# Layer 1's input projection: block sums of the token operand taken once in full precision, the token pairs in another order, and the products of a query group added straight from the accumulators

## The chip, the cores and the metric

The kernel runs on one NeuronCore of a Trainium2 chip. A core has a matrix engine (PE), a vector engine (DVE), an activation engine (ACT), a general-purpose engine (POOL) and a synchronisation engine (SP) that here issues nearly all transfers. Each engine works its own list of instructions in order; an instruction waits until what it reads is written and what it overwrites has been read. The metric is the device time of one execution in microseconds (us), the median of several.

## The reference, cut to what matters

Two layers run over 1024 latent tokens and 256 context tokens of width 1024. Layer 0 is windowed attention, layer 1 is multi-head latent attention. The change is in layer 1's input projection alone:

```python
hx = rms_norm(x, norm_g[i]) * (1.0 + scale_x[:, None]) + shift_x[:, None]
hc = rms_norm(ctx, norm_g[i]) * (1.0 + scale_c) + shift_c
...
cq, ckv, kr, g = jnp.split(h @ w_in, [B_Q_LORA, B_Q_LORA + B_KV_LORA, ...], axis=-1)
q  = (rms_norm(cq, q_norm) @ w_uq).reshape(b, n, B_HEADS, B_NOPE + B_ROPE)
kv = (rms_norm(ckv, kv_norm) @ w_ukv).reshape(b, n, B_HEADS, B_NOPE + B_V)
```

Everything is fp32. `h @ w_in` has 512 columns `cq` and 1024 columns of gate `g`, wanted for the latent tokens alone, and 256 + 32 columns `ckv` and `kr`, wanted for all 1280 tokens.

## The kernel before

**Products.** An fp32 operand is held as two rounded parts, high and low. `split` makes them: ACT casts the high part (L125), DVE or POOL subtracts it for the low part (L126). A product of two such operands is three matmuls, high by high, low by high and high by low (L130, L131, L132).

**The tiles.** The 1280 tokens are ten tiles of 128, in five pairs: pair 0 is context, pairs 1 to 4 are latent. For a pair, `norm_x` loads two tiles, takes their squares' sum on ACT (L231), the power on POOL (L233) and scales on DVE (L234); `turn_h` transposes on PE (L245), writes the shifted and scaled result in fp32 to a transposed tile `xt` (ACT, L249) and splits it (L253, L254) into the pair's part of `hT1`. `xt` comes from a ring of two buffers, `xtr`.

**The kv stage.** `kv_tile` runs 24 matmuls of 128x288 for a tile, then ACT squares (L1026), DVE forms the mean (L1027), POOL takes the power -1/2 (L1028), and DVE scales the result (L1064). Two tiles later PE transposes it (L1077), it is split and stored (L1081).

**The block products.** `cq` and `g` are worked out by a scheme of Strassen's kind (Winograd's form): the weight columns come in six groups of 256 (`groups`: 0 and 1 are `cq`, 2 to 5 are `g`), and a group is seven products P1 to P7 instead of eight. A product is 12 matmuls of 128x512 into one of eight PSUM banks. P1 and P2 use raw blocks on both sides (the token side is `halves`, which lies over `hT1`); P6, P5, P7 and P4 use sums of token blocks T2, T1, T3, T4 against S2, S1, S3 and the raw block A22; P3 uses S4. `Group.op` makes the weight side (sums on DVE, L1146 to L1160, then a split with the low part on POOL), and `Group.P` issues the products and their combination.

`t_sums` makes the token side: for pairs 1 and 3 behind tile 6 and for pairs 2 and 4 behind tile 8, each a quarter-set of 128x1024. It reads pair 3's or 4's fp32 `xt` and the high and low parts of pair 1's or 2's `hT1`:

```python
nc.vector.tensor_sub(X, X, a[0])          # L1099
nc.vector.tensor_sub(X, X, a[1])          # L1100
nc.vector.tensor_sub(Y, Y, X)             # L1101
put(T2, Y, nc.vector)                     # high L1096 (ACT), low L1097
put(T1, X, nc.gpsimd)
nc.gpsimd.tensor_sub(X, Y, a[0])          # L1104
nc.gpsimd.tensor_sub(X, X, a[1])          # L1105
...
nc.gpsimd.tensor_sub(Y, b[0], Y)          # L1109, later
nc.gpsimd.tensor_add(Y, Y, b[1])          # L1110
```

**After a product.** P1 is copied out (ACT, L1174), P6 added to it (DVE, L1180); P7 and P5 are copied to buffers (ACT, L1184 and L1188) and added there by POOL (L1189, L1190); P4 and P3 are added from their banks by DVE (L1195, L1200). `post` then applies silu and stores to `g1_d` (L1207, L1208), or stores to `cq_d` (L1213) and collects squares (ACT L1215 or L1218, POOL L1219) in `sqacc`.

**The norm of cq.** `latent_rms` sums the squares over the columns by matmuls (L1224), takes the mean (DVE, L1228) and the power (POOL, L1229) and spreads it by transposes (L1234). `latent_rows` loads `cq` again (L1242) and scales it (L1243). Then `qr_tile` (transposes L1260, stores L1264) and `qn_tile` (L1281 to L1285) make the queries; they share buffers (`qst`, `stg`, `ev`) with the weight loads of the stages around them, the last of these `b_w_ukv` (L1388). The rotary key is made there too (L1424 to L1432). From then on the attention units run.

**What sets the order.** The program is written in one stream; a scheduler of the framework, with costs of its own, makes from it a fixed list for each engine. Buffers are offsets in KB in three areas (`F`, `R`, and `arena_k` for the upper part of `R`), so two uses of one offset also order the instructions.

## Time and profile before

| what | value |
|---|---|
| time, median of 3 runs | 1603.81 us (1602.33 to 1604.04) |
| the profiled execution's own time | 1606.34 us |
| its span, first to last instruction | 1604.6 us (1.74 us lie outside) |
| granted PE clock, mean | 0.98 |
| PE busy | 1535.8 us, 96% of the span |
| DVE, ACT, POOL busy | 1040.7, 806.3, 851.2 us |

Layer 1's input projection, with the cq norm and the queries, lies between about 705 and 1000 us of the span. The profile's stretches show for each engine how long it was busy in each, with the granted clock of PE; a row of waits names the engine, the line, what it waited for, the sum, the count and the longest.

### The profile page before, as it was taken

The page shows a single profiled execution, that of the slowest core. Times are in us where ns is not written, and L with a number is a line of the kernel's source. Part 1 is how long each engine was busy: PE and PEld are TensorE (multiplying, and loading weights), DVE is VectorE, ACT ScalarE, POOL GpSimd, SP SyncE. Part 2 cuts the span into 40 slices and gives each one's busy share as a digit, 9 for nine tenths or more (in the row PEclk, how much of TensorE's full clock was granted, in tenths as well). Part 3 has the DMA queues.
Part 4 walks back from the last instruction along what each step waited for, and adds up shares of the span by engine and source line. Part 5 has one row for each costly group of instructions (what it writes and reads, how often), then busy time and mean ns, then how long its engine had stood idle before and what let it go on. Part 6 is the DMA issues. An engine that isn't in the chain of part 4 may idle for free. (4 is left out here: it accounts for less than half of the span.)

```text
span 1604.6 us, 25745 instructions
## 1 busy us (share of the span) xinstructions
PE 1535.8 (96%) x9190; PEld 1194.6 (74%) x9190; DVE 1040.7 (65%) x1748; ACT 806.3 (50%) x1552; POOL 851.2 (53%) x873
## 2 busy tenths in 40 slices
PE   7999999999999999998698999999999999999998
PEld 4988888887888888878577777666766766766587
DVE  3868996557777777766543442667677677667354
ACT  4333222377777777768433433455555555555321
POOL 1152212136554444544877562588688688689510
PEclk9999999999999999999798999999999999999999
DMA  9347673654343333245133477222333233244151
GB/s 329 101 155 226 193 209 118 205 145 112 93 135 96 93 97 92 80 146 169 40 112 121 148 244 244 93 76 86 81 88 90 67 95 96 67 129 117 62 170 66
DMA packets 157967, 204.01 MB, mean 127 GB/s; under 512 B 14592, under 2 KB 91904, under 8 KB 157840
## 3 DMA queue, kind: packets, MB, share of 16 engines
q1 hardware_dynamic: 156368, 200.48, 41.7%
q10 hardware_dynamic: 1472, 1.90, 0.4%
q8 instruction: 72, 1.18, 0.3%
q14 instruction: 55, 0.45, 0.1%
HBM read 151.46 MB, written 50.87 MB: 126 GB/s over the span
## 5 line engine op out<-in xcount | busy, mean ns | idle before, releaser
L130 PE MATMUL PB<-arena_r 128*128 128x512 f32 (+2 forms) x990 | 371.7, 377 | 11.7 <-ACT arena_r L125 5.0
L1568 POOL TENSOR_TENSOR arena_f<-arena_f 128x512 f32<-128x512 f32 x252 | 328.3, 1303 | 82.2 <-ACT arena_f L1560 65.4
L131 PE MATMUL PB<-arena_r 128*128 128x512 f32 (+2 forms) x958 | 355.0, 371 | 4.7 <-POOL arena_r L126 3.5
L132 PE MATMUL PB<-arena_r 128*128 128x512 f32 (+2 forms) x926 | 340.1, 368 | 0.0
L126 POOL TENSOR_TENSOR arena_r<-arena_f,arena_r 128x512 fp32r<-128x512 f32 x110 | 147.2, 1350 | 282.4 <-ACT arena_r L125 236.9
L130 PEld LDWEIGHTS PB<-arena_r 128*128 128x128 f32 x990 | 189.3, 192 | 48.4 <-ACT arena_r L125 6.5
L1560 ACT ACTIVATE arena_f<-PB 128x1024 f32<-128x1024 f32 x160 | 164.1, 1026 | 109.6 <-PE PB L1554 69.2
L1519 DVE TENSOR_REDUCE arena_f<-PB 128x1 f32<-128x1024 f32 x128 | 156.0, 1218 | 86.5 <-PE PB L1517 86.4
L131 PEld LDWEIGHTS PB<-arena_r 128*128 128x128 f32 x958 | 183.6, 192 | 34.1 <-POOL arena_r L126 4.0
L132 PEld LDWEIGHTS PB<-arena_r 128*128 128x128 f32 x926 | 177.1, 191 | 28.9 <-issue 1.7
L1554 PE MATMUL PB<-arena_r 64*128 64x512 f32 (+1 forms) x1490 | 194.5, 392 | 0.3 <-ACT arena_f L1560 0.3
L1554 PEld LDWEIGHTS PB<-arena_r 64*128 64x128 f32 (+1 forms) x1490 | 135.8, 185 | 29.1 <-ACT arena_f L1560 1.8
L126 DVE TENSOR_TENSOR arena_r<-PB,arena_r 128x512 fp32r<-128x512 f32 (+1 forms) x171 | 115.6, 684 | 60.7 <-ACT arena_r L125 60.0
L1576 PE MATMUL PB<-arena_f 128*64 128x512 f32 x640 | 144.4, 597 | 0.0
L628 DVE CUSTOM_DVE_ANT_0 arena_f<-PB,arena_f,small 128x640 f32<-128x640 f32 (+2 forms) x176 | 125.0, 721 | 20.0 <-PE PB L617 13.3
L631 ACT ACTIVATE arena_f<-arena_f,small 128x640 f32<-128x640 f32 (+2 forms) x160 | 119.5, 747 | 35.1 <-DVE small L628 32.1
L125 ACT CAST arena_r<-arena_f 128x512 fp32r<-128x512 f32 (+1 forms) x139 | 83.7, 618 | 86.5 <-DMA arena_f<-b_w_ukv 18.2
L125 ACT CAST arena_r<-PB 128x512 fp32r<-128x512 f32 (+1 forms) x171 | 98.1, 581 | 46.5 <-PE PB L648 44.2
L617 PE MATMUL PB<-arena_k,arena_r 128*128 128x256 f32 (+1 forms) x576 | 112.0, 309 | 2.5 <-DVE small L628 1.3
L648 PE MATMUL PB<-ident,arena_f 128*128 128x128 f32 x672 | 104.6, 275 | 1.1 <-DVE arena_r L126 0.7
L1576 PEld LDWEIGHTS PB<-arena_f 128*64 128x64 f32 x640 | 43.1, 136 | 83.2 <-issue 79.7
L617 PEld LDWEIGHTS PB<-arena_k,arena_r 128*128 128x128 f32 x576 | 89.8, 189 | 15.2 <-DVE small L628 3.7
(253 smaller groups left out, 2693.0 us busy)
## 6 DMA issues: line engine op xcount, KB each, us to landing
arena_f<-ada_w SPq DMA_DIRECT2D x40, 512.0 KB, 4.8
arena_r<-q_d SPq DMA_DIRECT2D x80, 256.0 KB, 3.9
arena_r<-qn_d SPq DMA_DIRECT2D x64, 256.0 KB, 4.1
arena_r<-qr_d SPq DMA_DIRECT2D x170, 64.0 KB, 3.4
arena_f<-a_w_in SPq DMA_DIRECT2D x40, 256.0 KB, 3.1
g_d<-arena_f SPq DMA_DIRECT2D x32, 256.0 KB, 2.8
q_d<-arena_f SPq DMA_DIRECT2D x64, 128.0 KB, 2.5
arena_f<-b_w_in SPq DMA_DIRECT2D x16, 512.0 KB, 3.8
```

What stands on the lines that cost most here:

```text
L125: nc.scalar.copy(hi, src)
L126: (lo_eng or nc.vector).tensor_sub(lo, src, hi.bitcast(F32))
L130: nc.tensor.matmul(o, ah, bh, start=first, stop=False, skip_group_check=more)
L131: nc.tensor.matmul(o, al, bh, start=False, stop=False, skip_group_check=more)
L132: nc.tensor.matmul(o, ah, bl, start=False, stop=last, skip_group_check=more)
L617: nc.tensor.matmul(S[:, at : at + n], qT[:, s, hq, :], kT[:, g, k : k + n], start=s == 0, stop=s == 1)
L628: nc.vector.tensor_tensor_reduce(P[:, a:b], S[:, 256 + a : 256 + b], mk, 1.0, sk, ALU.add, ALU.min, to)
L1519: nc.vector.reduce_max(mx[:, 32 + b : 33 + b], flat, AX.X, negate=True)
L1554: nc.tensor.matmul(S[:, t], k[r, c : c + 128], q[r], start=j == 0, stop=j == 4)
L1560: nc.scalar.activation(E, self.S, AF.Exp)
L1568: eng.tensor_add(self.acc, self.acc, E[:, t])
L1576: nc.tensor.matmul(self.pv[p : p + 64], Vq[:, cs[t], self.h % 4, :], E[:, t], start=i == 0, stop=i == 4)
```

## The change

- **Pairs.** The kv stage takes the pairs in the order 0, 1, 3, 2, 4. The sums of pairs 1 and 3 are written behind the fourth tile, those of pairs 2 and 4 behind the eighth. Pair 2's `xt` takes the buffer of pair 1's, pair 4's that of pair 3's.
- **Sums.** They are taken from two fp32 `xt`, one subtraction each (L1093, L1094, L1095, L1102), high parts on ACT (L1098), low parts on DVE (L1099). POOL has no part in them. T4's split comes later, as before.
- **First products.** P1 and P2 of groups 0 and 1, which need no sums, stand ahead of all products that do; those of groups 2 and 3 stand inside the kv stage, as before. The weight side runs eight products ahead (six before), and loads for P1 and P2 alone fetch half.
- **Combination.** Within a group the order is 6, 5, 7, 4, 3. DVE adds P5 and P7 straight from their banks (L1177); the ACT copies and the POOL adds are gone.
- **The norm of cq.** `latent_rms` stands behind group 4's second product (before: group 2's second). The loads of `cq` (L1226) are written ahead of the scaling (L1232), which is split by halves of the tokens.
- **Weights and buffers.** The last query weights' low parts go to DVE; `stg` has five slots there that share nothing with `qst`; many offsets in `F` are others.

By number the lines behind it move up: L1027 and L1028 become L1026 and L1027, L1064 L1065, L1077 L1078, L1174 L1165, L1180 L1171, L1195 and L1200 L1185, L1219 L1205, L1224 to L1234 L1210 to L1220. The lists of PE hold the same matmuls in another order; ACT's has 26 rows fewer, POOL's 30 fewer, DVE's 18 more.

POOL at the end of the kv stage. In the names, `arena_f` and `arena_r` are the areas, `small` holds one value per token, `krF` the rotary key. Before:

```order
L126 TENSOR_TENSOR arena_r<-arena_f,arena_r 128x512
L1097 TENSOR_TENSOR arena_r<-arena_f,arena_r 128x4x256
L1104 TENSOR_TENSOR arena_f<-arena_f,arena_r 128x1024
L1105 TENSOR_TENSOR arena_f<-arena_f,arena_r 128x1024
L1028 TENSOR_TENSOR small<-small 128x1
L291 TENSOR_TENSOR krF<-krF,arena_f 128x32
L1109 TENSOR_TENSOR arena_f<-arena_r,arena_f 128x1024
L126 TENSOR_TENSOR arena_r<-arena_f,arena_r 128x512
L1028 TENSOR_TENSOR small<-small 128x1
L1110 TENSOR_TENSOR arena_f<-arena_f,arena_r 128x1024
```

And at the same place of the change:

```order
L126 TENSOR_TENSOR arena_r<-arena_f,arena_r 128x512
L1027 TENSOR_TENSOR small<-small 128x1
L291 TENSOR_TENSOR krF<-krF,arena_f 128x32
L1027 TENSOR_TENSOR small<-small 128x1
L291 TENSOR_TENSOR krF<-krF,arena_f 128x32
L126 TENSOR_TENSOR arena_r<-arena_f,arena_r 128x512 x4
L1027 TENSOR_TENSOR small<-small 128x1
L291 TENSOR_TENSOR krF<-krF,arena_f 128x32
```

The sums between the powers are gone; ahead of the power of the ninth tile stand four low parts of weights.

DVE at the same place of the change, from the second set of sums on:

```order
L1094 TENSOR_TENSOR arena_f<-arena_f 128x1024
L1099 TENSOR_TENSOR arena_r<-arena_f,arena_r 128x4x256
L1095 TENSOR_TENSOR arena_f<-arena_f 128x1024
L1099 TENSOR_TENSOR arena_r<-arena_f,arena_r 128x4x256
L1102 TENSOR_TENSOR arena_f<-arena_f 128x1024
L1099 TENSOR_TENSOR arena_k<-arena_f,arena_k 128x4x256
L1026 TENSOR_SCALAR small<-small 128x1
L126 TENSOR_TENSOR arena_k<-PB,arena_k 128x256
L1065 SCALAR_TENSOR_TENSOR arena_f<-PB,small,arena_f 128x256
L281 TENSOR_TENSOR krF<-PB,arena_f 128x32
L286 TENSOR_TENSOR arena_f<-PB,arena_f 128x2x8 x2
L1099 TENSOR_TENSOR arena_k<-arena_f,arena_k 128x4x256
```

Six of the sums' instructions stand in a row ahead of the mean (L1026) and the scaling (L1065) of one tile, and another low part ahead of the next tile's.

POOL around the power for the cq norm, before (L1229) and now (L1215):

```order
L1219 TENSOR_TENSOR arena_f<-arena_f 128x512
L126 TENSOR_TENSOR arena_r<-arena_f,arena_r 128x512
L1219 TENSOR_TENSOR arena_f<-arena_f 128x512
L126 TENSOR_TENSOR arena_r<-arena_f,arena_r 128x512
L1229 TENSOR_TENSOR small<-small 128x8
```

```order
L126 TENSOR_TENSOR arena_r<-arena_f,arena_r 128x512
L1205 TENSOR_TENSOR arena_f<-arena_f 128x512
L126 TENSOR_TENSOR arena_r<-arena_f,arena_r 128x512 x12
L1215 TENSOR_TENSOR small<-small 128x8
L126 TENSOR_TENSOR arena_r<-arena_f,arena_r 128x512 x9
```

Between the last sum of squares and the power stood one low part; now there are twelve.

The core of the diff:

```diff
@@ -986,21 +986,20 @@
-    xtr = Ring(F, [22, 30], 2048)
-    ev = Ring(F, [2, 4, 6, 8], 512)
...
-    cmb = Ring(F, [10 + 2 * i for i in range(6)], 512)
...
-    stg = Ring(F, [42, 44.25, 49.5], 576)
...
+    xr = Ring(F, [22, 26, 45], 1024)
+    xtr = Ring(F, [14, 37], 2048)
+    wr = Ring(F, [30, 32], 512)
...
+    ov = Ring(F, [34, 45, 47, 4, 6], 512)
...
+    stg = Ring(F, [30, 32.25, 49.5], 576)
@@ -1085,45 +1086,35 @@
-    def t_sums(p, xt):
...
+    def t_sums(x0, x1, cs, t4):
+
+        la, lb, ha, hb = x0[:, 0:4], x0[:, 4:8], x1[:, 0:4], x1[:, 4:8]
+        sub = nc.vector.tensor_sub
+        sub(la, ha, la)
+        sub(ha, hb, ha)
+        sub(hb, hb, la)
+
+        def put(T, src):
             nc.scalar.copy(T[:, 0, :, cs], src)
...
+            sub(T[:, 1, :, cs], src, T[:, 0, :, cs].bitcast(F32))
+
+        put(T2, hb)
+        sub(t4, lb, hb)
+        put(T1, la)
+        put(T3, ha)
+        return lambda: put(T4, t4)
@@ -1178,43 +1169,38 @@
-            if n == 7:
-                self.p7 = cmb.next()
-                self.product(self.a, self.S3, tt(T3), True)
-                nc.scalar.copy(self.p7, self.a)
...
+                self.c22 = self.p1
+            if n in (5, 7):
+                ps, A, T = (self.b, self.S1, T1) if n == 5 else (self.a, self.S3, T3)
+                self.product(ps, A, tt(T), True)
+                c = ov.next()
+                nc.vector.tensor_add(c, ps, self.c22)
+                if self.c22 is not self.p1:
+                    self.post(1, 1, c)
+                self.c22 = c
...
@@ -1234,15 +1220,17 @@
+    def load_rows(h):
+        rows = [cqr.next() for c in range(4)]
+        for c, u in enumerate(rows):
+            load(out=u, in_=cq_d[c, :, 512 * h : 512 * h + 512])
+        return rows
...
@@ -1289,86 +1277,87 @@
+    rest5 = (6, 5, 7, 4, 3)
+    todo = [(0, (1, 2)), (1, (1, 2))] + [(i, rest5) for i in range(4)]
+    todo += [(4, (1, 6, 5, 7, 2, 4, 3)), (5, (1, 6, 2, 5, 7, 4, 3))]
...
+    order1 = [2 * p + j for p in (0, 1, 3, 2, 4) for j in range(2)]
...
-        if ti in (6, 8):
-            t_rest.append(t_sums(ti // 2, xts[ti // 2]))
...
+        if i == 3:
+            t_rest.append(t_sums(xts[1], xts[3], slice(0, 256), t4buf))
+        if i == 7:
+            t_rest.append(t_sums(xts[2], xts[4], slice(256, 512), xts[2][:, 4:8]))
...
-            if gi == 2 and i == 1:
+            if gi == 4 and i == 1:
                 latent_rms()
+            if gi == 4 and i == 5:
+                rows = [load_rows(0)]
+            if last and i == 1:
+                rows.append(load_rows(1))
...
-                stg = Ring(F, [22, 24, 30], 512)
+                stg = Ring(F, [8, 10, 12, 22, 24], 512)
                 fetch1(3)
...
+            if last and i in (4, 5):
+                scale_rows(i - 4, rows[i - 4])
+    fetch1(4, nc.vector)
+    ev = Ring(F, [34, 45, 47, 6], 512)
+    rtmp = Ring(F, [49, 2], 512)
+    qst = Ring(F, [14, 18, 30, 37, 41, 26], 1024)
```

More of the change, by code (lines that the diff above doesn't have):

```diff
@@ L1031 @@
     fetch1(0, nc.vector)
+    xts = {}
     for p in range(2):
         xs = [norm_x(src1(2 * p + j), xr, junk) for j in range(2)]
-        turn_h(p, xs, shp(xtr.next(), 8, 256), hT1[p], ada1, range(4))
+        xts[p] = shp(xtr.next(), 8, 256)
+        turn_h(p, xs, xts[p], hT1[p], ada1, range(4))
     load2(out=cosb, in_=t["cos_b"].rearrange("p (t d) -> p t d", t=8))
@@ L1205, in post @@
             if self.kind == "g":
-                out = self.c11 if (i, half) == (0, 0) else c
+                out = ov.next() if (i, half) == (0, 0) else c
                 nc.scalar.activation(out, c, AF.Silu)
@@ L1210, in post @@
             if (i, half) == (0, 0):
-                nc.scalar.copy(self.c11, c)
-                c = self.c11
+                out = ov.next()
+                nc.scalar.copy(out, c)
+                c = out
             load(out=cq_d[ch, :, ts], in_=c)
@@ L1216, in post @@
                 return
-            sq = ev.next()
+            sq = ov.next()
             nc.scalar.activation(sq, c, AF.Square)
@@ L1235, in latent_rms, with scale_rows @@
             nc.scalar.copy(r_b[h], pt)
-    def latent_rows():
-        ts = []
-        for h in range(2):
-            for c in range(4):
-                u = cqr.next()
-                load(out=u, in_=cq_d[c, :, 512 * h : 512 * h + 512])
-                nc.vector.scalar_tensor_tensor(u, u, qncol[:, c : c + 1], r_b[h], ALU.mult, ALU.mult)
-                ts.append((h, c, u))
-        return ts
+    def load_rows(h):
[3 more added lines that the diff above has]
+        return rows
+    def scale_rows(h, rows):
+        ts = slice(512 * h, 512 * h + 512)
+        for c, u in enumerate(rows):
+            nc.vector.scalar_tensor_tensor(u, u, qncol[:, c : c + 1], r_b[h], ALU.mult, ALU.mult)
+            split(cqT[0][:, c, ts], cqT[1][:, c, ts], u)
     def qr_tile(ti):
@@ L1322 @@
             if n % 2:
[L1323 removed]
+                turn_h(p, xs, xt, hT1[p], ada1, (2, 3))
             if n + 1 < NT:
[L1325 removed]
+                nx = norm_x(src1(order1[n + 1]), xr, junk)
         flush(2)
[L1327 to L1333 removed]
@@ L1334 @@
-    order = [(1, 2, 6, 7, 5, 4, 3), (1, 6, 7, 5, 2, 4, 3), (6, 7, 5, 4, 3), (6, 7, 5, 4, 3)]
-    order += [(1, 6, 7, 5, 2, 4, 3), (1, 6, 2, 7, 5, 4, 3)]
-    def operands():
-        for g, ns in zip(groups, order):
-            if g is not groups[0]:
-                g.fetch()
-            for n in ns:
-                if g is groups[0] and n < 3:
-                    continue
-                g.op(n)
-                yield
-    ops = operands()
-    for _ in range(6):
+        if i == 3:
+            t_rest.append(t_sums(xts[1], xts[3], slice(0, 256), t4buf))
@@ L1349 @@
+        if i == 7:
+            t_rest.append(t_sums(xts[2], xts[4], slice(256, 512), xts[2][:, 4:8]))
+        if i in (5, 7):
+            g = groups[2 + i // 7]
+            g.P(1)
+            g.P(2)
+            if i == 7:
+                wslot.i = 0
+                next(ops)
+                next(ops)
+    flush()
+    next(ops)
+    next(ops)
+    wr = Ring(F, [30, 26], 1024)
+    for _ in range(4):
         next(ops)
-    for gi, g in enumerate(groups):
+        if t_rest:
+            t_rest.pop(0)()
@@ L1351 @@
+    for gi, ns in todo:
+        g = groups[gi]
         last = gi == 5
-        if gi not in (2, 3):
-            g.p1 = cmb.next()
-            g.c11 = ev.next()
-        for i, n in enumerate(order[gi]):
+        for i, n in enumerate(ns):
             g.P(n)
             next(ops, None)
-            if gi == 2 and i == 1:
+            if gi == 4 and i == 1:
                 latent_rms()
+            if gi == 4 and i == 5:
+                rows = [load_rows(0)]
+            if last and i == 1:
+                rows.append(load_rows(1))
@@ L1360 @@
             if last and i == 2:
-                rows = latent_rows()
-                stg = Ring(F, [22, 24, 30], 512)
+                stg = Ring(F, [8, 10, 12, 22, 24], 512)
                 fetch1(3)
-            if last and i == 3:
-                for j, (h, c, u) in enumerate(rows):
-                    ts = slice(512 * h, 512 * h + 512)
-                    split(cqT[0][:, c, ts], cqT[1][:, c, ts], u)
-    fetch1(4)
-    ev = Ring(F, [2, 4, 6, 8], 512)
-    rtmp = Ring(F, [10, 12], 512)
```

113 lines of the change are left out of this document (37 added, 76 removed).

## The prediction

> **What bounds the kernel now.** I read the page first. PE does not only lead, it is nearly full:
>
> ```profile
> PE 1535.8 (96%) x9190; PEld 1194.6 (74%) x9190; DVE 1040.7 (65%) x1748; ACT 806.3 (50%) x1552; POOL 851.2 (53%) x873
> PEclk9999999999999999999798999999999999999999
> ```
>
> The matmuls stay the same, so only PE's idle time and its half clock can be won. The clock's digits fall below 9 just at slices 20 and 22 (40.1 us each): 762 to 802 us and 842 to 883 us, both inside the changed stage. So I cut that stage into stretches next:
>
> ```profile
> 705.00:740.00 35.00, 30.21 (x178) 26.66 (x178) 19.96 (x43) 24.65 (x54) 10.22 (x14) 0.90 0.62 203
> 740.00:782.00 42.00, 37.47 (x240) 34.10 (x239) 28.02 (x57) 31.43 (x68) 22.98 (x20) 0.96 0.32 98
> 782.00:806.00 24.00, 9.78 (x27) 6.96 (x26) 13.92 (x19) 6.37 (x11) 21.46 (x13) 0.66 0.13 39
> 806.00:847.00 41.00, 39.93 (x172) 32.06 (x171) 21.18 (x21) 16.45 (x30) 32.36 (x25) 0.99 0.42 123
> 847.00:862.00 15.00, 10.18 (x39) 8.28 (x38) 6.15 (x9) 4.66 (x9) 11.00 (x9) 0.66 0.47 140
> 862.00:929.00 67.00, 65.34 (x288) 53.80 (x287) 23.66 (x30) 28.74 (x53) 40.52 (x32) 1.00 0.49 152
> 929.00:937.00 8.00, 4.57 (x16) 3.50 (x15) 4.56 (x10) 1.20 (x2) 4.97 (x4) 0.79 0.69 254
> 937.00:978.00 41.00, 40.49 (x196) 32.80 (x195) 15.25 (x30) 13.80 (x25) 19.10 (x15) 1.00 0.83 249
> 978.00:988.00 10.00, 7.23 (x21) 5.40 (x20) 3.49 (x6) 5.05 (x12) 3.16 (x3) 0.66 0.78 234
> ```
>
> Columns: the stretch, its length, PE's busy time and count, weight loads, DVE, ACT, POOL, granted clock, DMA share, GB/s. What a stretch loses against a PE that is busy at full clock is its length less busy time times clock. In order: A (705) 35 − 30.21 × 0.90 = 7.8; B (740) 6.0; C (782) 24 − 9.78 × 0.66 = 17.5; D (806) 1.5; E (847) 15 − 10.18 × 0.66 = 8.3; F (862) 1.7; G (929) 4.4; the next 0.5; H (978) 5.2. Together 53 us. POOL is busy 21.46 of C's 24 us. A product at full clock: 172 matmuls in D's 39.93 us, 0.23 us each, so 12 take 2.8 us; one of 288 columns, by width, 0.13.
>
> Who ends PE's waits, 705 to 1000 us (sum, count, longest):
>
> ```profile
> PE PB L1077 <- DVE arena_f L1064: 5.7, 1, 5.7
> PE PB L130 <- ACT arena_r L125: 5.0, 1, 5.0
> PE PB L131 <- POOL arena_r L126: 4.0, 2, 3.5
> PE PB L1224 <- POOL arena_f L1219: 3.9, 2, 3.3
> PE PB L1260 <- POOL arena_f L291: 3.9, 2, 3.4
> PE PB L245 <- DVE arena_f L234: 3.3, 4, 1.3
> PE PB L1424 <- DVE arena_r L1432: 2.8, 1, 2.8
> PE PB L130 <- ACT arena_f L1174: 1.8, 2, 1.7
> ```
>
> The first three are C's, the fourth E's, the fifth G's, the seventh H's. The long ones cost twice, since PE comes out of them at half clock. Starts of two neighbours in C are 0.42 us apart:
>
> ```profile
> 789.39 0.63 PE L132 MATMUL PB<-arena_r 128*128 128x512 f32 x1
> 789.81 0.63 PE L130 MATMUL PB<-arena_r 128*128 128x512 f32 x1
> ```
>
> **The change part by part: the sums (C).** POOL between 745 and 806 us, then DVE:
>
> ```profile
> L126 POOL TENSOR_TENSOR arena_r<-arena_f,arena_r 128x512 fp32r<-128x512 f32 x5 | 6.4, 1275 | 0.0
> L1097 POOL TENSOR_TENSOR arena_r<-arena_f,arena_r 128x1024 fp32r<-128x1024 f32 x2 | 6.2, 3090 | 0.0
> L1105 POOL TENSOR_TENSOR arena_f<-arena_f,arena_r 128x1024 f32<-128x1024 f32 x2 | 5.7, 2858 | 0.1
> L1028 POOL TENSOR_TENSOR small<-small 128x1 f32<-128x1 f32 x6 | 3.3, 550 | 6.0 <-DVE small L1027 6.0
> ...
> L1097 DVE TENSOR_TENSOR arena_k<-arena_f,arena_k 128x1024 fp32r<-128x1024 f32 x4 | 7.0, 1773 | 0.0
> L1101 DVE TENSOR_TENSOR arena_f<-arena_f 128x1024 f32<-128x1024 f32 x2 | 5.7, 2872 | 0.0
> L1064 DVE SCALAR_TENSOR_TENSOR arena_f<-PB,small,arena_f 128x256 f32<-128x256 f32 x6 | 2.9, 484 | 16.4 <-POOL small L1028 16.4
> L1099 DVE TENSOR_TENSOR arena_f<-arena_f,arena_r 128x1024 f32<-128x1024 f32 x2 | 2.4, 1222 | 0.0
> ```
>
> After the second bar stands the engine's idle time before such instructions, and what ended it. L1064's is the reading: DVE idled 16.4 us for a power of 0.55 us that stood in POOL's list behind sums of about 3 us. The change takes five such instructions a set off POOL (one L1097 and four sums), some 14.5 us, 29 for both. What is left for PE to wait on in C, four terms:
>
> (1) The ninth tile's scaled result. Behind its last matmul at least: ACT's square (0.39, row below) and cast (0.62), a low part on POOL 1.28, the power 0.55, the scaling 0.48: 3.3. At most, ACT's cast of a sum 1.05 and DVE's low part 1.77 also lie between: 5.4 with the smaller DVE rows. PE covers it by the tenth tile, 24 × 0.13 = 3.1. So 0.2 to 2.3; I take 1.2.
>
> (2) P6 of group 0, which needs T2 and S2. From the second set's start DVE has three sums and five low parts, 3 × 1.22 + 5 × 1.77 = 12.5 us if POOL does not slow it, 17.5 at L1101's 2.87 for a sum; then three weight sums of 0.7 to 1.58 (L1160's row below), an ACT cast and a POOL low part: 17 to 24 us. In PE's new list 60 matmuls of products and 56 of the kv stage stand between, 60 × 0.23 + 56 × 0.13 = 21.1, about 22 with transposes. P1 and P2 of group 1, now ahead of P6, are 24 of the 60, 5.5 us. So 0 to 2, and up to 4 where DVE stops for the kv tiles in between; I take 2.
>
> (3) Half clock behind either: 12 matmuls at 0.42 instead of 0.23 are 2.3; with at least one wait of this length likely, 2.0.
>
> (4) P2 waits for P1's copy out of the same bank where no other product stands between, as in groups 0 and 1; before, 1.8 at two places (L1174's row): 0.6.
>
> Left 5.8 of 17.5 (0 to 9): **−11.7**.
>
> ```profile
> L1026 ACT ACTIVATE arena_f<-PB 128x256 bf16<-128x256 f32 x10 | 3.9, 389 | 4.2 <-PE PB L132 4.1
> L125 ACT CAST arena_r<-arena_f 128x512 fp32r<-128x512 f32 x11 | 6.8, 620 | 24.8 <-DMA arena_f<-b_w_ukv 18.2 <-DMA arena_f<-b_w_uq 6.6
> L1096 ACT CAST arena_r<-arena_f 128x1024 fp32r<-128x1024 f32 x4 | 4.2, 1051 | 10.4 <-POOL arena_f L1105 9.4 <-DVE arena_f L1100 0.9
> L1160 DVE TENSOR_TENSOR arena_f<-arena_f 128x512 f32<-128x512 f32 x6 | 9.5, 1582 | 14.4 <-POOL arena_r L126 14.4
> L1195 DVE TENSOR_TENSOR arena_f<-PB,arena_f 128x512 f32<-128x512 f32 x6 | 4.1, 687 | 9.9 <-PE PB L132 9.9
> ```
>
> On term (3) the Trainium skill can be set against the row. Its page "TensorE: Matmul & The Clock Gate", section "What's actually happening", says the clock falls to half after an idle window of about 3.4 us and rises after a busy one. By that rule, waits of 1 to 2 us would carry no half clock and the sum would be 2 us better. The trace disagrees: H's wait is 2.8 us long, and H's clock is 0.66. I keep the 2.0.
>
> **Pairs and buffers (A, B).** The second set's transposed tiles wait for the buffers of the first set's. The first set is eight DVE instructions, 4 × 1.22 + 4 × 1.77 = 12 us, of which the two kv tiles between cover 6.3 and products of groups 2 and 3 the rest. B's other waits (norm, L245 on L234) stay or grow behind a DVE sum of 1.2 to 2.9: **+1** (0 to 8, the rival below). In A the first loads of the layer take offsets that layer 0 still uses: **+1** (0 to 2).
>
> **Combination (D, F).** DVE takes two adds a group, 12 × 0.69 (L1195's row) = 8.3 us, in a stage where it is busy 21 of 41 us (D). POOL loses two adds a group:
>
> ```profile
> L1189 POOL TENSOR_TENSOR arena_f<-arena_f 128x512 f32<-128x512 f32 x6 | 8.7, 1449 | 6.7 <-ACT arena_f L1188 6.6
> 855.63 1.65 POOL L1229 TENSOR_TENSOR small<-small 128x8 f32<-128x8 f32 x1 [0.52 <-DVE small L1228]
> L1243 DVE SCALAR_TENSOR_TENSOR arena_f<-arena_f,small 128x512 f32<-128x512 f32 x8 | 7.5, 946 | 10.7 <-DMA arena_f<-cq_d 10.5
> L281 DVE TENSOR_TENSOR arena_f<-PB,arena_f 128x512 f32<-128x512 f32 x8 | 5.5, 685 | 11.8 <-DMA g_d<-arena_f 8.1 <-PE PB L132 3.7
> ```
>
> On PE's path the new add is seen where P4 follows P7 into the same bank; at 0.69 it is hidden by half a product. If DVE is late, each costs its lateness: **+1** (0 to 4).
>
> **The cq norm (E, F).** E's 8.3 us are PE waiting 3.3 for the last sum of squares in POOL's list, 0.9 for the power, and the half clock behind. Twelve products later the sums of squares (six of 1.4 us) are long done: that wait goes. What comes is the power itself behind up to twelve low parts on POOL. They are needed by products that lie ahead, so POOL should have worked them off, but the power can only begin when PE's sums and DVE's mean are there, and takes 1.65; six matmuls, 1.4 us, cover it. Left are about 0.8 of wait, the slower clock 1.2, and 1.0 for DVE's scaling (L1243's new line) ahead of an add: 3 of 8.3 + 1.7 (0 to 8): **−7.0**. F's wait of DVE for the `cq` loads, 10.5 us, has its loads issued earlier now.
>
> **The queries (G, H).** G stays: the first query tile's buffer is again that of a late gate store (L281's row, 8.1), so 0. In H ACT waits 18.2 us for `b_w_ukv` (L125's row above) through a three-slot ring whose offsets the query buffers share; five slots of their own remove the sharing, not the traffic, 249 GB/s at 0.83 DMA share ahead of H. I keep 2.2 of 5.2 (0 to 5): **−3.0**.
>
> Sum: −11.7 − 7.0 − 3.0 + 1 + 1 + 1 = −18.7. Against the profiled execution's own time, 1606.34 (span 1604.6 and 1.74 outside), that is 1587.6. It was 2.53 above the median shown, so I predict **1585 us**.
>
> **The rivals.** *The gains of E and H come back elsewhere.* For it: DMA at 0.83 ahead of H, and the twelve low parts ahead of the power, up to 12 × 1.28 = 15 us if not worked off. Against: POOL idles 51 us for casts in the stage, it has room. Then 7 of the 10 are lost: 1592.
>
> *DVE's sums are slowed by POOL's low parts.* For it: L1101 beside POOL 2.87, L1099 alone 1.22. Each of five instructions ahead of P6 held by one 1.28 low part makes 6.4 us: 1591. Against: POOL has only six low parts there. The Trainium skill, "SBUF — State Buffer", section "SBUF: two separate sides", gives the rule: DVE and POOL share a port pair that one holds for a whole instruction while the other stops. By that rule the slowing is at most one POOL instruction for each start, which is this rival; L1101's extra 1.65 agrees with a stop behind part of a 2.85 us neighbour.
>
> *More is won.* POOL is free in B too, so its powers there come at once, and terms (1) to (3) are hidden: 5.8 + 1 + 6 of B's and E's rests: 1572.
>
> *The burst on DVE turns into the bound (slower).* Eight instructions at rows beside POOL are 4 × 2.87 + 4 × 1.77 = 18.6 us. If the cover is the two kv tiles alone (6.3), pair 2's transposes wait some 9 to 12 us for the ring's slot, pair 4's the same, each with 2.3 of half clock, and C keeps 9 instead of 5.8: 1585 + 2 × 11 + 3 = 1610. It is slower than before once each wait passes 8 us. Against: low parts of products fill PE there, and POOL, the slowing neighbour, is the engine that is emptied.
>
> *PE gains nothing*, because the scheduler's list already puts each wait's cover elsewhere: 1603.
>
> **How the numbers follow.** Forecast 0.49 (its own range 1577 to 1590); less from E and H 0.17; DVE slowed 0.10; more won 0.12; slower 0.08; nothing 0.04. About 0.2%, 3.2 us, is what a measurement of this kernel can tell from no change. Faster: the first four, 0.88; same 0.04; slower 0.08. The range leaves out the slower and unchanged cases and the far end of the larger gain: 1571 to 1599; its lower end is the larger gain, its upper end has C's rest at 9 and E's at 8 together (1585 + 3.2 + 5 = 1593) with B's upper bound nearly full.
>
> **What would show it.** Right: in C, no wait of PE on L1065 above 2.5 us and a stretch's clock above 0.9; no wait at L1210 above 1 us; DVE's idle before L1065 for the power well under 16.4 us. POOL's busy time falls by 29 + 17 us (the sums; 12 adds of 1.4). Wrong: a wait at L245 or L249 for DVE's L1099 above 5 us in B; PE waiting at L1220 for POOL's L1215 above 3 us; P6's first matmul waiting above 4 us for T2; H's wait for `b_w_ukv` as long as before.

## The result, and the profile after

| | median | lowest to highest | runs |
|---|---|---|---|
| before | 1602.33 us | 1598.89 to 1604.04 | 5 |
| changed | 1591.68 us | 1590.05 to 1595.18 | 5 |

The ratio is 0.9942, 95% interval 0.9919 to 0.9964: the change gains 10.65 us, 0.7%. Forecast were 18.7 us and 1585, with 1571 to 1599 as the range. The profiled execution of the changed kernel took 1591.68 us itself, its span is 1590.0 us.

PE is as full as it was, POOL lost 42 us of busy time (851.2 before), and the low digits of the clock lie elsewhere. By the page's counts POOL has 26 instructions fewer than before, ACT 12 fewer and DVE 20 more; the figures given with the change count rows of the lists. From the page:

```profile
PE 1528.5 (96%) x9190; PEld 1189.0 (75%) x9190; DVE 1040.6 (65%) x1768; ACT 801.4 (50%) x1540; POOL 809.3 (51%) x847
PEclk9999999999999999998989999999999999999999
```

The two profiled executions differ by 14.7 us, more than the medians. Part of this is no effect of the change. The last transposes of layer 0, in code that the change leaves alone, in the timeline of PE before:

```profile
700.56 0.38 PE L677 MATMUL PB<-ident,arena_f 128*128 128x128 f32 x2
```

and after:

```profile
696.35 0.38 PE L677 MATMUL PB<-ident,arena_f 128*128 128x128 f32 x2
```

4.2 us lie ahead of the changed stage. In the profiles of the experiments below, which leave that code alone too, the same row lies anywhere between 695.33 and 699.70 us, so I count the 4.2 us as scatter. The layers' ends can be compared in the same way: the first attention matmul of layer 1 starts at 999.27 before,

```profile
999.27 0.73 PE L1517 MATMUL PB<-arena_r 64*128 64x512 f32 x4
```

and at 984.76 now, 14.5 us earlier:

```profile
984.76 0.50 PE L1506 MATMUL PB<-arena_r 64*128 64x512 f32 x2
```

So the stage itself gained 14.5 − 4.2 = 10.3 us, which is what the medians gained. Since PE runs the same matmuls, I could follow the difference through the stage by the starts of the matmul with the same number in both traces (the first of 288 columns, then the 72nd, 84th, ... of 512 columns); their order differs between the kernels, their widths do not. The stretches' letters are those of the prediction:

| part | forecast, us | measured, us |
|---|---|---|
| A, start of the layer | +1 | −1.1 |
| B, kv stage to its last matmul | +1 | −0.4 |
| C, end of the kv stage to the sums' first products | −11.7 | −13.3 |
| combination in the groups (D, and on through F) | +1 | +24.5 |
| E and F, the cq norm and its rows | −7.0 | −12.2 − 2.0 + 4.1 = −10.1 |
| G and H, the queries | −3.0 | −10.0 |
| sum | −18.7 | −10.4 |

The total came out inside the range because two errors of opposite sign met: one term was mis-sized by 23.5 us, and the other terms together came out 15 us better than forecast. Nearly all of the 24.5 us lies at the five waits of the first row below and the half clock behind them; P6's wait of 1.8 us, a term of C in the forecast, falls into that row of the table too. The waits of PE from 700 to 1000 us show the large one in the first row:

```profile
PE PB L130 <- DVE arena_f L1177: 14.1, 5, 4.2
PE PB L1078 <- DVE arena_f L1065: 4.2, 1, 4.2
PE PB L245 <- ACT arena_f L249: 2.9, 2, 2.7
PE PB L130 <- DVE small L1026: 2.9, 1, 2.9
PE PB L131 <- POOL arena_r L126: 1.8, 1, 1.8
PE PB L1248 <- POOL arena_f L291: 1.6, 1, 1.6
PE PB L1220 <- POOL small L1215: 1.1, 1, 1.1
```

Of C's three waits before (5.7, 5.0, 3.5 us) the first has only shrunk, to the 4.2 us of the second row; the other two, both of P6, have become the 1.8 us at L131. Of E's, the one for the sum of squares is gone, and the one for the power is 1.1 us (0.9 before). New are five for L1177, the new add of P5 and P7. The stretches by busy time say the same (columns as in the prediction): 795 to 842 us loses 47 − 40.38 × 0.89 = 11 us, where the like stretch D of before lost 1.5.

```profile
776.00:795.00 19.00, 13.05 (x53) 10.02 (x52) 11.41 (x22) 8.52 (x18) 13.72 (x12) 0.91 0.54 151
795.00:842.00 47.00, 40.38 (x158) 32.36 (x158) 19.27 (x24) 13.53 (x23) 27.73 (x22) 0.89 0.43 130
928.00:985.00 57.00, 57.00 (x285) 47.40 (x285) 23.98 (x45) 21.74 (x43) 24.39 (x22) 1.00 0.75 242
```

What does the new add wait for? Not for PE. Here is DVE between 802 and 810 us, start, duration, and the idle time before with what ended it:

```profile
802.53 0.68 DVE L1177 TENSOR_TENSOR arena_f<-PB,arena_f 128x512 f32<-128x512 f32 x1
806.28 0.69 DVE L1143 TENSOR_TENSOR arena_f<-arena_f 128x512 f32<-128x512 f32 x1 [3.07 <-POOL arena_r L126]
808.74 0.69 DVE L1137 TENSOR_TENSOR arena_f<-arena_f 128x512 f32<-128x512 f32 x1 [1.77 <-DMA arena_f<-b_w_in]
809.35 0.68 DVE L1177 TENSOR_TENSOR arena_f<-PB,arena_f 128x512 f32<-128x512 f32 x1
```

The first L1177 is P5's add, the last one P7's. Between them stand L1143 and L1137, weight sums for later groups, and DVE takes its list in order. The chain that ended last follows it back (start, duration, what):

```profile
803.76 1.26 POOL arena_r L126
805.03 3.68 DMA arena_f<-b_w_in
808.74 0.06 DVE arena_f L1137
...
809.35 0.69 DVE arena_f L1177
...
810.09 0.79 PE PB L130
```

Read upwards: PE's P4 may not write the bank until P7's add has read it; the add stands behind L1137; L1137 needs a load of weights that takes 3.68 us, the last 1.77 of which DVE stands idle; and the load was issued when POOL had split the old weights in one of the two weight buffers. Four of the five waits are of 2.4 us or more, and behind each of these PE ran 8 to 14 matmuls at half clock.

### The profile page after: what moved, and what is told of

The parts are those of the page before. It is cut to its first block, busy times and chain, and to the rows that moved or that the text cites. A ratio compares the mean times of both kernels' runs of the same rounds, so it can differ in the third digit from the quotient of the medians.

```text
span 1590.0 us, 25744 instructions
## 1 busy us (share of the span) xinstructions
PE 1528.5 (96%) x9190; PEld 1189.0 (75%) x9190; DVE 1040.6 (65%) x1768; ACT 801.4 (50%) x1540; POOL 809.3 (51%) x847
## 4 chain that ended last, share of the span: by engine, by line
PE 72%; DVE 8%; issue 5%; DMA 5%; POOL 5%; ACT 4%; SPq 1%; DVEq 0%; POOLq 0%; ACTq 0%
PE PB L1543 11%; PE PB L130 11%; PE PB L131 10%; PE PB L132 10%; PE PB L1565 8%; PE PB L1506 4%; PE PB L617 4%; PE PB L658 4%; PE PB L648 4%; POOL arena_r L126 2%; DVE arena_f L195 2%; DVE arena_f L515 1%; ACT arena_r L125 1%; PE PB L1514 1%; DMA arena_f<-a_w_in 1%
## 5 line engine op out<-in xcount | busy, mean ns | idle before, releaser
L131 PE MATMUL PB<-arena_r 128*128 128x512 f32 (+2 forms) x958 | 352.7, 369 | 1.2 <-POOL arena_r L685 0.8
L126 POOL TENSOR_TENSOR arena_r<-arena_f,arena_r 128x512 fp32r<-128x512 f32 x106 | 148.4, 1412 | 308.1 <-ACT arena_r L125 251.5
L131 PEld LDWEIGHTS PB<-arena_r 128*128 128x128 f32 x958 | 182.5, 190 | 30.0 <-DVE arena_r L420 2.3
L126 DVE TENSOR_TENSOR arena_r<-PB,arena_r 128x512 fp32r<-128x512 f32 (+1 forms) x171 | 115.7, 684 | 61.0 <-ACT arena_r L125 60.2
L125 ACT CAST arena_r<-arena_f 128x512 fp32r<-128x512 f32 (+1 forms) x139 | 83.2, 618 | 106.8 <-PE PB L132 38.0
L125 ACT CAST arena_r<-PB 128x512 fp32r<-128x512 f32 (+1 forms) x171 | 98.1, 581 | 46.3 <-PE PB L648 44.1
```

The lines of the kernel that those rows point to most:

```text
L125: nc.scalar.copy(hi, src)
L126: (lo_eng or nc.vector).tensor_sub(lo, src, hi.bitcast(F32))
L131: nc.tensor.matmul(o, al, bh, start=False, stop=False, skip_group_check=more)
```

## Experiments

Each kernel's ratio is against runs of the kernel before on the same chip, as the change's 0.9942. Differences from the change are told by these ratios, and where they are too close, by the traces alone.

**P7 copied out by ACT.**

```diff
+                if n == 7:
+                    nc.scalar.copy(c, ps)
-                nc.vector.tensor_add(c, ps, self.c22)
+                nc.vector.tensor_add(c, c if n == 7 else ps, self.c22)
```

> The changed kernel with one addition: ACT copies P7 out of its bank into the buffer where the sum goes, and DVE adds from that buffer (the added step of the change undone for P7 alone, P5 still straight from its bank). Theory A (PE's 14.1 us of waits for L1177 come from where P7's add stands in DVE's list, behind the next group's weight sums, which wait for buffers and for the weights' load): the bank is freed by ACT, these waits fall below 3 us in all, the stretch runs at full clock, and the time is 1572 to 1580 us. Rival B (the add itself is too slow, its 0.69 us and the way there): the copy takes as long as the add, about 0.6 us, the waits stay above 8 us, 1588 to 1593 us. Rival C (the whole weight side is late, and PE waits for it under another name): the waits move to PE's L130 and L131 for ACT's L125 and POOL's L126, above 8 us, 1588 to 1593 us.

Measured: 1583.46 us, ratio 0.9879 (0.9862 to 0.9897). PE's waits for the add, which is L1179 here, fell from 14.1 to 2.5 us. Two waits for ACT came in, for the copy itself (L1178) and for P1's copy (L1165):

```profile
PE PB L130 <- ACT arena_f L1178: 3.4, 1, 3.4
PE PB L130 <- ACT arena_f L1165: 2.7, 1, 2.7
PE PB L130 <- DVE arena_f L1179: 2.5, 2, 1.6
```

What theory A says of the waits held, rivals B and C are out: a copy of 0.6 us does not hold PE, and the weights themselves are not late. The time missed A's range by 3 us, because ACT's list has weight casts ahead of its copies: a part of the wait moved to another list.

**P7 ahead of P5.**

```diff
-    rest5 = (6, 5, 7, 4, 3)
+    rest5 = (6, 7, 5, 4, 3)
...
-    todo += [(4, (1, 6, 5, 7, 2, 4, 3)), (5, (1, 6, 2, 5, 7, 4, 3))]
+    todo += [(4, (1, 6, 7, 5, 2, 4, 3)), (5, (1, 6, 2, 7, 5, 4, 3))]
```

> The changed kernel with P7 ahead of P5 in every group, as before the change: P5's product then lies between P7 and P4, which share a bank, and P4's between P5 and P3. Theory A: each of the five waits of 4.2, 2.7, 2.4, 0.9 and 3.7 us gets a product of 2.8 us as a cover in place of half of one (1.4 us), so each falls by 1.4 at least: 14.1 becomes about 7 us or less, and 1578 to 1586 us. Rival B (the add alone is slow): covered in full, no waits at all, 1570 to 1577 us. Rival C (weight side late): the waits for L1177 vanish but as much comes at L130 and L131 for L125 and L126, 1588 to 1593 us.

Measured: 1588.96 us, ratio 0.9916 (0.9897 to 0.9936).

```profile
PE PB L130 <- DVE arena_f L1177: 6.4, 3, 2.5
PE PB L1248 <- POOL arena_f L291: 5.0, 1, 5.0
PE PB L130 <- ACT arena_f L1165: 3.2, 2, 1.9
```

The waits for the add fell to 6.4 us, as A had it, but the time was 3 us above A's range: a wait of 5.0 us at the first query tile (1.6 in the change) and P1's copy took most of it back. A longer cover hides the add's lateness, it doesn't remove it.

**Six buffers for the weight sums.**

```diff
-    sr = Ring(F, [8, 10, 12], 512)
+    sr = Ring(F, [8, 10, 12, 14, 16, 18], 512)
...
+            if i == 4:
+                sr = Ring(F, [8, 10, 12], 512)
```

> The changed kernel with six buffers for the weight sums in place of three, for groups 0 to 3 (three for groups 4 and 5 as now). It takes away the first of the two things that DVE stands for ahead of P7's add: L1143 waiting for POOL's L126 (9.9 us of the 17). The other, L1137 waiting for the weights' load (7.0 us), is left. Theory A: PE's waits for L1177 in the first three groups, 4.2, 2.4 and 2.7 us, shrink by about half, the half clock behind two of them goes, 1580 to 1587 us; DVE still waits for the load at L1137. Rival B: no change, 1589 to 1594 us. Rival C: no change in the time, since DVE's sums are not what is late.

Measured: 1592.55 us, ratio 0.9937 (0.9921 to 0.9953): no change. DVE's wait at L1143 fell from 9.9 to 3.8 us, and the one at L1137 for the load rose from 7.0 to 15.8, so that the add came as late as ever. DVE's waits from 785 to 915 us, and below them PE's:

```profile
DVE arena_f L1137 <- DMA arena_f<-b_w_in: 15.8, 5, 4.7
DVE arena_f L1143 <- POOL arena_r L126: 3.8, 2, 2.5
...
PE PB L130 <- DVE arena_f L1177: 14.2, 5, 4.3
```

The expectation of A that half would go was wrong: the two waits don't add, the first one lay wholly in the shadow of the load.

**Three buffers for weight halves, five for sums.**

```diff
-    sr = Ring(F, [8, 10, 12], 512)
+    sr = Ring(F, [8, 10, 12, 14, 16], 512)
...
-    wr = Ring(F, [30, 26], 1024)
+    wr = Ring(F, [30, 26, 18], 1024)
```

> The changed kernel with three buffers for the halves of a group's weights in place of two and five for the weight sums in place of three, for groups 0 to 3. Both things that DVE stands for ahead of P7's add become earlier: the load can be issued while the group before still holds its second half. Theory A: PE's waits for L1177 in the first three groups (9.3 us of the 14.1, about 17 with half clock) mostly go, the one ahead of the query stage (3.7 us) stays: 1574 to 1582 us. Rival B: no change, 1589 to 1594 us. Rival C: PE's waits move to L130 and L131 for L125 and L126, 1586 to 1593 us.

Measured: 1585.11 us, ratio 0.9892 (0.9876 to 0.9907); PE's waits for L1177 11.4 us in four, of which 6.5 lie in the first three groups (9.3 before). A group has two halves, so with three buffers every other load still waits: DVE's longest wait at L1137 was 4.4 us. The direction is A's, the size less.

**Four buffers for weight halves.**

```diff
+            if i == 4:
+                wr = Ring(F, [30, 26], 1024)
...
-    wr = Ring(F, [30, 26], 1024)
+    wr = Ring(F, [30, 26, 14, 18], 1024)
```

> The changed kernel with four buffers for the halves of a group's weights in place of two, for groups 0 to 3, three buffers for the sums as now. Theory A (after the run with six sum buffers, in which PE's waits stayed at 14.2 us and DVE's wait only moved to the load: what P7's add stands behind is the weights' load): the load of a group is issued a group earlier, DVE's wait at L1137 for it falls below 2 us in all, PE's waits for L1177 in the first three groups (9.3 us) fall below 2, the one at 907 us stays: 12 to 16 us faster than the change, 1576 to 1580 us. Rival B (the sums' buffers and POOL are the limit after all): L1143 keeps waiting for POOL, PE's waits stay above 6 us, 1585 to 1592 us.

Measured: 1580.23 us, ratio 0.9856 (0.9835 to 0.9877), 0.2 us above A's range. From 700 to 1000 us PE waits for L1177 5.5 us in four, 4.0 of it the last one; in the groups from 795 to 860 us it is 0.5. PE's waits in this stretch, then DVE's at L1137 from 795 to 905 us:

```profile
PE PB L130 <- DVE arena_f L1177: 0.5, 2, 0.4
...
DVE arena_f L1137 <- DMA arena_f<-b_w_in: 1.8, 1, 1.8
```

This ties the first three groups' loss to the load: with two buffers more the add isn't late. One thing came along with the edit. The scheduler made another list for DVE, in which L1137, the sum that reads the fresh load, stands ahead of P5's add already, and only L1143 is left between P5's add and P7's. The earlier load and the place of L1137 are therefore not told apart. Of the kernels here that compute the reference this one has the lowest ratio, 0.9% under the change's and 1.4% under the kernel before.

**Buffers of their own for group 1's half-width weights.**

```diff
+    wr = Ring(F, [26, 28], 512)
     next(ops)
     next(ops)
     wr = Ring(F, [30, 26], 1024)
```

> The changed kernel with two more buffers for the half-width weights of group 1's P1 and P2, which now wait until POOL has split group 0's. Theory A (the ninth tile's wait, L1078 for L1065, 4.2 us at 776 us, comes from POOL's list: the power of that tile stands behind two low parts of weights whose load waited for a buffer until 771.9 us): the load is issued earlier, the power comes before PE needs it, the wait falls below 1.5 us and the half clock behind it goes: 4 to 6 us faster than the change, 1585 to 1588 us. Rival B (DVE's run of sums is what is late: the mean L1026 stands behind L1099, until 778.5 us): the wait stays above 2.5 us, 1589 to 1593 us.

Measured: 1593.57 us, ratio 0.9934 (0.9913 to 0.9955): no change, and 0.6 us above rival B's range. The wait fell by less than a microsecond; PE's wait, and the power of that tile on POOL in this kernel:

```profile
PE PB L1078 <- DVE arena_f L1065: 3.3, 1, 3.3
...
779.48 0.55 POOL L1027 TENSOR_TENSOR small<-small 128x1 f32<-128x1 f32 x1 [2.36 <-DVE small L1026]
```

Rival B holds here: POOL now stands idle for 2.36 us until DVE's mean comes, so the 3.3 us that are left come from DVE's run of sums ahead of the mean. In the change both lists were late: POOL's power started at 779.63 us, behind its low parts, and the mean had ended only 1.0 us earlier:

```profile
778.46 0.14 DVE L1026 TENSOR_SCALAR small<-small 128x1 f32<-128x1 f32 x1
```

**The last query weights' low parts on POOL.**

```diff
-    fetch1(4, nc.vector)
+    fetch1(4)
```

> The changed kernel with the low parts of the last query weights on POOL again, as before the change (one step undone). Theory A (the last wait for L1177, 3.7 us at 907 us, comes from P7's add standing in DVE's list behind these low parts, which wait for ACT's casts and these for the load of b_w_uq): that wait goes with its half clock, about 5 us, and nothing else: 1585 to 1588 us. Rival B (the low parts were moved since POOL is late there): PE waits for POOL at the first query tile instead, by 3 us or more, 1589 to 1594 us.

Measured: 1596.56 us, ratio 0.9958 (0.9943 to 0.9972); by the ratio's interval it isn't told apart from the change, by the trace it is worse. The wait it was to remove grew from 3.7 to 5.5 us, since other low parts on DVE, ahead of P7's add, wait 5.0 us for ACT:

```profile
PE PB L130 <- DVE arena_f L1177: 16.1, 5, 5.5
...
DVE arena_k L126 <- ACT arena_r L125: 5.0, 1, 5.0
```

A's place was right (DVE's list), its cause wrong: what is late is ACT's casts behind the loads of `b_w_uq`, and this kernel leaves them as they are. B's wait at the first query tile didn't come either, it is 2.1 us.

**The three together.** The edits of the last three paragraphs together:

> The changed kernel with the three above together: buffers of their own for group 1's half-width weights, four buffers for the weight halves of groups 0 to 3, the last query weights' low parts on POOL. Theory A: the three gains add, 5 + 14 + 5: 1566 to 1572 us, and what is left of PE's waits between 700 and 1000 us is below 14 us (28.9 in the change). Rival B (they share a cause downstream, such as POOL's or SP's list, so the second hides the third): 1574 to 1582 us.

Measured: 1583.28 us, ratio 0.9872 (0.9857 to 0.9887), no better than the four buffers alone and 1.3 us above B's range. Nothing added up, as two of the three gain nothing: the last wait for L1177 is 5.6 us as with the low parts on POOL, the one at L1078 3.2.

**The cq norm back behind group 2's second product.**

```diff
-            if gi == 4 and i == 1:
+            if gi == 2 and i == 1:
                 latent_rms()
```

> The changed kernel with the cq norm's sums and power back behind group 2's second product (one step undone). Theory A (the later place is what removes the 8.3 us of the stretch around 847 us): PE waits for POOL's sum of squares L1205 and the power L1215 again, 4 us or more with half clock behind: 6 to 10 us slower than the change, 1598 to 1602 us. Rival B (it is POOL's relief from the sums and the combination's adds that made the squares come in time, the place matters little): no wait at L1210 above 1 us, within 3 us of the change, 1589 to 1595 us.

Measured: 1587.41 us, ratio 0.9895 (0.9878 to 0.9911): *faster* than the change, by 0.5%, outside both theories' ranges. There is no wait at L1210 at all, and the one for the power is short. PE's waits, then POOL's from 820 to 846 us:

```profile
PE PB L1220 <- POOL small L1215: 0.7, 1, 0.7
...
POOL arena_r L126 <- ACT arena_r L125: 7.2, 2, 4.5
```

The starts of like matmuls say where it gains: up to the 228th it runs as the change does (0.4 us apart), then it loses 3.7 us at the norm, gets them back and 1.7 us more where the change waits for L1177 in the next group (2.7 us there, 0.2 here), and gains 5.4 us where the change has its own norm. So in this kernel the later place costs some 7 us. E's loss of before went without it. The difference most likely lies on POOL, for it has sums of squares, power and low parts in its list, and waits for work (7.2 us of 26) where before it was the engine that PE waited for. This is an argument from the trace: which of the things taken off POOL did it was not tried one by one.

**Three query weight buffers on the old offsets.** One of them lies over a row of `cq` that is still to be scaled, so this kernel computes those queries from overwritten values; it runs as many instructions.

```diff
-                stg = Ring(F, [8, 10, 12, 22, 24], 512)
+                stg = Ring(F, [22, 24, 30], 512)
```

> The changed kernel with three weight buffers for the query weights in place of five, the offsets as before the change, one of them shared with the query buffers (one step undone). Theory A (the 5.8 us won around 980 us come from the five buffers): ACT waits for b_w_ukv again, PE waits at L1413 or the products behind it for 2 us or more with half clock behind: 4 to 7 us slower than the change, 1595 to 1599 us. Rival B (the loads come earlier because the list on SP and the free low parts on POOL changed): no such wait, 1589 to 1594 us.

Measured: 1593.54 us, ratio 0.9932 (0.9917 to 0.9948), as the change, as B had it. But the trace shows A's wait come back, and a gain that hides it:

```profile
PE PB L130 <- DVE arena_f L1177: 10.6, 4, 4.3
PE PB L1248 <- POOL arena_f L291: 4.9, 2, 3.1
PE PB L1413 <- DVE arena_r L1421: 1.9, 1, 1.9
```

In the starts of like matmuls the stretch of the queries costs 8.8 us more than in the change (2.2 at the first tile, 2.9 over the tiles, 3.7 at the rotary key), and the last wait for L1177 is gone, 5.5 us less. Another 2.8 us less are chance as far as the runs tell: behind the third wait for L1177, 2.80 us here and 2.74 in the change, PE ran at full clock here and at half clock there. The five buffers do what they should in H; three of them are those of the weight sums, so the loads of `b_w_uq` come later and hold ACT's casts and with them P7's last add.

**T1's and T3's low parts on POOL.**

```diff
-        put(T1, la)
-        put(T3, ha)
+        put(T1, la, nc.gpsimd.tensor_sub)
+        put(T3, ha, nc.gpsimd.tensor_sub)
```

> The changed kernel with the low parts of T1 and T3 on POOL in place of DVE (four instructions of 128x1024 in all; the subtractions stay on DVE). Theory A (what PE lost at the end of the kv stage came from powers standing behind 128x1024 instructions on POOL): the power of the ninth tile stands behind one or two of them again, the wait L1078 for L1065 grows from 4.2 to 6 us or more: 2 to 6 us slower than the change, 1594 to 1598 us. Rival B (in the changed kernel DVE's run of sums is the later of the two, and four instructions less of 1.3 to 2.3 us bring the scaling forward): the wait falls below 3 us, 1586 to 1591 us.

Measured: 1595.61 us, ratio 0.9944 (0.9929 to 0.9959), not told apart from the change by the time. By the trace the end of the kv stage is worse, and the middle too, where a norm's scaling (L234) waits for POOL:

```profile
PE PB L245 <- DVE arena_f L234: 6.1, 2, 5.7
PE PB L1078 <- DVE arena_k L126: 5.8, 1, 5.8
```

5.8 us against 4.2 at L1078 and 5.7 against 1.6 at L245. A's direction, a little under its 6 us; B's gain did not come. The power of the ninth tile started at 784.22 us, 2.4 us behind the mean, for a low part of a sum and one of weights stood ahead of it on POOL. Since the time does not show it, this is support from one trace.

**Four weight buffers with three more steps.** P7 two products ahead of P4 in groups 4 and 5, the second set of sums written two tiles later, and group 1's small buffers. In group 5, P2 then comes behind the query weights that are written over a token block it reads, so it reads other values; the instructions are the same.

```diff
-    todo += [(4, (1, 6, 5, 7, 2, 4, 3)), (5, (1, 6, 2, 5, 7, 4, 3))]
+    todo += [(4, (1, 6, 7, 5, 2, 4, 3)), (5, (1, 6, 7, 5, 2, 4, 3))]
...
-        if i == 7:
+        if i == 9:
             t_rest.append(t_sums(xts[2], xts[4], slice(256, 512), xts[2][:, 4:8]))
```

> The kernel with four buffers for the weight halves (the fastest so far, 1580.2 us), and three things more: P7 two products ahead of P4 in group 5 and group 4, the second set of sums written behind the tenth tile in place of the eighth (one of DVE's low parts then stands behind the ninth tile's mean), and group 1's half-width weights in buffers of their own. Theory A (DVE's list is what PE waits for, at 897 us behind the query rows' low parts, at 780 us behind the sums): the wait for L1177 of 4.0 us falls below 1, the one at L1078 of 4.1 below 2: 6 to 9 us faster than with the four buffers alone, 1571 to 1575 us. Rival B (other waits take their place: P1's copy on ACT, the first query tile's buffer): 1577 to 1583 us.

Measured: 1577.48 us, ratio 0.9826 (0.9812 to 0.9841).

```profile
PE PB L1248 <- POOL arena_f L291: 6.2, 1, 6.2
PE PB L1078 <- DVE arena_f L1065: 3.4, 2, 2.1
PE PB L130 <- DVE arena_f L1177: 0.8, 3, 0.4
```

The waits for the add are gone everywhere, 0.8 us of 14.1, so theory A holds for the last group too. They are covered rather than removed, since P4 now comes two products behind P7. The wait at L1078 fell to 3.4 us, not below 2. The time is rival B's: the first query tile now waits 6.2 us for its buffer (a gate store), and by the intervals of the two ratios the kernel isn't told apart from the one with four buffers alone. As it stands this is a look at the list, not a version to use.

## Why the prediction was right, and where it was not

**C, right in the engine and near in size, but not by the wait it was read from.** Forecast −11.7 with 5.8 left; measured −13.3. The reading held: DVE idled for a short power behind long sums on POOL, and its idle time before the scaling fell from 16.4 to 3.5 us (739 to 795 us):

```profile
L1065 DVE SCALAR_TENSOR_TENSOR arena_f<-PB,small,arena_f 128x256 f32<-128x256 f32 x7 | 3.4, 483 | 3.5 <-POOL small L1027 3.5
```

PE gained little by that, though: its wait for the scaling fell from 5.7 to 4.2 us. The larger part came from P6's two waits. P6 needs both parts of S2, and before these stood behind the same sums on POOL by two other ways: ACT's cast of the high part (L125) stood behind the cast of a sum that waited 9.43 us for POOL's L1105, and POOL's low part (L126) stood behind L1109 and L1110, until 801.5 us.

```profile
796.00 1.04 ACT L1096 CAST arena_r<-arena_f 128x1024 fp32r<-128x1024 f32 x1 [9.43 <-POOL arena_f L1105]
797.84 0.64 ACT L125 CAST arena_r<-arena_f 128x512 fp32r<-128x512 f32 x1
801.52 1.26 POOL L126 TENSOR_TENSOR arena_r<-arena_f,arena_r 128x512 fp32r<-128x512 f32 x1
```

The change also put P1 and P2 of group 1 ahead in the list, so that P6 comes 24 matmuls later. How much is due to the sums and how much to this order no run tells apart; that low parts of 128x1024 on POOL delay the power again shows in one trace (T1's and T3's low parts on POOL).

Of its terms, (1) was too small: PE's wait is 4.2 us, forecast 1.2 with 2.3 as the upper bound. The rows named for that bound add up to 6.1 us, not 5.4, which would make it 3.0. It also counted one DVE low part ahead of the mean, where the list has three sums and three low parts, and these ran until 778.5 us, when PE had been through with the tenth tile for 2 us. (2) was near: P6 waits 1.8 us, forecast 2, though for POOL's low part of the weights and not for T2.

**The combination, the step that failed.** Its working set 12 adds of 0.69 us against DVE's idle share and found the add "hidden by half a product". The add's length is right, 0.685 us. Missing was what the add stands *behind*: weight sums in DVE's list, waiting for loads. Before, ACT copied P7 out of its bank, and DVE's waits in the groups cost PE next to nothing: DVE then waited 16.8 and 14.4 us at L1152 and L1160, for POOL's low parts, while PE had no wait for a DVE add between 806 and 929 us.

```profile
DVE arena_f L1152 <- POOL arena_r L126: 16.8, 5, 5.6
```

One warning stood in that trace. P3's add (L1200, 905.41 us) came behind a scaling (L1243) that waited 5.37 us for a load of `cq`; ACT's list waited for that add, and PE 1.66 us for ACT's copy of P1 behind it (L1174). The change put more work that PE waits for into a list that waits. This term was +24.5 with half clock, bounds 0 to 4. The copy shows the place, P7's add in DVE's list; six sum buffers against four weight buffers show that the load was what it stood behind, with the reservation on the list made there.

**The cq norm, right sign by a wrong reason.** Forecast −7.0 from the later place; measured −10.1. The old wait went for 12.2 us, but undoing the later place gains time. The step failed where it assumed that at the old place the squares would come as late as before; with the rest of the change in place there was no wait for them (L1210) there at all.

**G and H, undersized.** Forecast −3.0, measured −10.0: the first tile's wait fell from 3.4 to 1.6 us, and in H no wait of 2 us is left, where 2.2 us had been set aside for DMA traffic. The stretch from 928 to 985 us is full, 57.00 of 57 us at a clock of 1.00, with 0.75 DMA share: the traffic was no limit. That the shared buffers were is what the kernel with three of them bears out, 8.8 us in this stretch.

**A, B.** Forecast +1 each, measured −1.1 and −0.4. The buffer waits expected in B came (2.7 us at L245 for L249), others went.

**The rivals.** The slower one named the right engine, DVE, and a wait that came, for the ring's slot, but at the wrong size: its burst of sums held PE for 2.7 us there and 4.2 at the ninth tile, not 9 to 12. The rival that POOL's low parts slow DVE's sums came true in part, ahead of the ninth tile instead of P6: of the six instructions there three took 2.3 us and three 1.2 to 1.3, and POOL ran low parts of weights beside the slow ones. That is 3.2 us ahead of the mean; how much of it reached PE was not tried. None of the rivals had the price of the combination. Of the signs of being right one failed, PE's wait on L1065 (4.2 us, not below 2.5). The total lay inside the range because the errors had opposite signs, not because the sum's terms were right.

**Half clock.** The rule of the Trainium skill, "TensorE: Matmul & The Clock Gate", section "What's actually happening" (half clock after an idle window of about 3.4 us), was set aside for the row of H. The changed kernel's trace bears that out in part: behind a wait of 2.42 us, shorter than the rule's window, PE ran at half clock, 0.42 us from start to start.

```profile
829.35 0.63 PE L132 MATMUL PB<-arena_k,arena_r 128*128 128x512 f32 x1
829.77 0.63 PE L130 MATMUL PB<-arena_k,arena_r 128*128 128x512 f32 x1
```

Behind the 1.77 us at 793.33 it did not, 0.23 us apart. Here the trace agrees with what the prediction drew from the rule for waits of 1 to 2 us. The half clock of term (3) came behind the ninth tile's wait, which was 4.2 us long. The length alone does not decide in these runs. In the kernel with three query weight buffers PE stayed at full clock behind 2.80 us,

```profile
849.08 0.40 PE L132 MATMUL PB<-arena_k,arena_r 128*128 128x512 f32 x1
849.31 0.40 PE L130 MATMUL PB<-arena_k,arena_r 128*128 128x512 f32 x1
```

and fell to half clock, 0.43 us apart, behind 1.90 us at 970.07.

## What to carry to other kernels

Before you move a short instruction that another engine waits for onto a less busy engine, read what stands ahead of it in that engine's list and what *that* waits for: idle share is not availability when the idle time is waiting in order. A wait that costs nothing becomes a cost as soon as something critical is queued behind it; the cheapest cure here was not to move the instruction back but to start the load earlier (two more buffers, some 14 us by the ratios, with another list for DVE). And undo each part of a change by itself: here a part with a plausible reason, the later norm, cost 7 us inside a change that won.

## What the runs showed of the hardware that was not expected

PE fell to half clock after waits as short as 1.90 us (three query weight buffers, 970.07 us) and kept full clock after waits as long as 3.26 us (buffers for group 1's weights, 780.61 us), so a single wait's length does not tell its price; the same wait cost 2.8 us more in one kernel than in another by this. Two waits in a row on one engine did not add up: with more buffers for sums DVE waited 6 us less for POOL and 9 us more for the load, and PE's wait stayed at 14.1 to 14.2 us. Profiled executions differ by up to 5.2 us at a point ahead of which the kernels run the same code (695.33 to 700.56 us), so a stage's gain is better read from a common start than from two spans.
